# Attention heads of a two-layer trunk: f32 matmuls replaced by three passes on split parts

## The chip, the cores and the metric

The kernel runs on one core of a Trainium2 chip. The metric is the device time of one launch in microseconds. Before the change three runs took 1253.34, 1255.0 and 1253.88 us; the median is 1253.88.

## What is computed

The reference runs two layers over 256 tokens of width 2048. Layer 0 is a Mamba-2 block, layer 1 a sparse attention with a lightning indexer; behind each stands `x = LayerNorm(alpha * x + mixer(x))`. The change touches only the attention of layer 1:

```
q     = (c_q @ w_uq).reshape(b, L, 32, 128)
q_lat = einsum('bthd,hcd->bthc', q, w_uk)
...
logits = einsum('bthc,btkc->bthk', q_lat, kv_sel) * 128 ** -0.5     # selected keys only
pr     = softmax(where(valid, logits, -inf))
o_lat  = einsum('bthk,btkc->bthc', pr, kv_sel)
o      = einsum('bthc,hcv->bthv', o_lat, w_uv).reshape(b, L, 4096)
return (o * silu(gate)) @ w_out
```

There are 32 heads of 128 channels. The kernel computes per head the keys `c_kv @ w_uk` and the values `c_kv @ w_uv`, and a mask stands for the selection.

## The kernel before, in words

The core has a matrix engine (TensorE, PE in the profile; its weight loads are PEld), a vector engine (VectorE, DVE), a scalar engine (ScalarE, ACT), GpSimd (POOL) and a queue of loads (SyncE, SP). Tiles lie in SBUF with 128 partitions. Matmuls write to PSUM, which this kernel divides into eight banks of 512 f32 per partition: three banks tagged `acc`, two `y`, two `m`, one `s`.

All weights pass through one stream of units (class `Stream`, lines 65 to 133). A unit is 128 x 1024 f32 values, loaded by SP into `raw`. ACT copies it to `hi`, rounded to the format fp32r (L98); DVE subtracts, `lo = raw - hi` (L106). Activations are split in the same way. A product is then three single-pass matmuls: hi by hi, hi by lo, lo by hi. `run` (lines 120 to 127) converts up to unit i + 3, issues the matmuls of unit i, and then advances every side generator by one step, older generators first. Each engine executes its instructions in the order in which this loop writes them, so `yield` counts units: a step behind n yields is written n units later. A new tile with the tag of an old one takes the place of one that is no longer used; its writer waits for the last reader of what stood there.

The heads run in 16 pairs. For pair p there are two units and after them units of gates:

- `pair_a` (lines 811 to 831): keys and values of two heads, 12 matmuls each of 256 columns, into two `acc` banks.
- `pair_b` (lines 833 to 844): queries of two heads, 24 matmuls of 256 columns, into a third `acc` bank.
- gates (`add_gate`, line 672, with `stream_w`, line 269): two units per head's gate, 16 matmuls each, into an `acc` bank. `halves` (line 289) takes it out: an ACT copy, and one unit later a DVE addition (L292). The loop at lines 909 to 919 writes one gate after pairs 0, 2, 4, ... and two after pairs 1, 3, 5, ...

So two pairs make ten units. The 32 gates are spread: eight are written before the heads, 24 among them. `gate_steps` (lines 661 to 670) keeps them in a tile with 12 buffers, from the gate's computation to the head that uses it.

`evac_steps` (lines 846 to 851) copies keys, values and queries from PSUM to f32 tiles `hk`, `hv`, `hq` with three buffers each, on ACT, right behind their unit. `head_steps` (lines 853 to 905) is one generator per head. Head 2p starts two units after `pair_b`, head 2p + 1 five units after it:

- its first step: logits in f32, a `y` bank, two matmuls (128 x 128 by L857 and 128 x 256 by L858; the upper right block is masked and left out)
- one unit later: DVE adds the mask and takes the extremum (L866); two: ACT takes the exponential (L871); three: DVE normalises (L874, L876)
- five: TensorE transposes the probabilities to an `m` bank (L882); six: ACT copies them to `prT` (L885)
- eight: outputs in f32, a `y` bank, two matmuls (256 and 128 columns, L889 and L891); nine: DVE multiplies by the gate (L895); then ACT and DVE split the product for the last projection (L902, L904)

Ahead of the heads the indexer's work (lines 748 to 806) lies in an area `sC` of 8192 f32 per partition: latents, indexer queries `qx`, scores `sc` and others, of which lines 1028 to 1039 cut off pieces by `area`. Its last step is the top-k search on DVE (`top_steps`, L793 and L794), which still runs while the first pair of heads is computed. Behind the heads, `x1_steps` (lines 1061 to 1073) loads two rows of gains in pieces into tiles with the tags `hk` and `hq`.

Of the kernel before, what the change touches and what calls it, by code (L numbers as in the profile page):

```python
# [9 lines left out]
F32 = mybir.dt.float32  # L10
F32R = mybir.dt.float32r
I32 = mybir.dt.int32
AF = mybir.ActivationFunctionType
# [3 lines left out]
P = 128  # L17
T = 256
# [29 lines left out]
RAW = 4  # L48
SPLIT = 4
DT_AT = 2  # L50
ON_ACT = 1
EARLY = 8
HELD = 6
# [83 lines left out]
def trunk_kernel(ctx: ExitStack, tc: tile.TileContext, x, xt, w1, wdt, dtp, prm, wo1,  # L137
                 wkv, wcq, wix, wg, wab, wo2, lnr, out):
    nc = tc.nc
# [13 lines left out]
    v = nc.vector  # L153
# [4 lines left out]
    def y_tile(name):  # L158
        return p_y.tile([P, 512], F32, tag="y", name=name)

    def m_tile(name):
        return p_m.tile([P, 512], F32, tag="m", name=name)
# [126 lines left out]
    def halves(dst, ps):  # L289
        nc.scalar.activation(dst, ps[:, T:2 * T], AF.Copy)  # L290
        yield
        v.tensor_add(dst, ps[:, 0:T], dst)  # L292
        yield
# [60 lines left out]
    def m_steps(g, c):  # L354
# [3 lines left out]
        for k in range(2):  # L358
            hh = g * 8 + 2 * c + k
            e = sp3.tile([P, 384], F32, tag="E", name=f"E{hh}")  # L360
            for s, o in ((0, 0), (1, 256)):
                src, dst = a[:, k, s * P:T], e[:, o:o + T - s * P]
                if k < ON_ACT:
                    nc.scalar.activation(dst, src, AF.Relu, scale=-1.0, bias=ask[:, s, hh:hh + 1])  # L364
# [5 lines left out]
        for k, e in enumerate(es):  # L370
            nc.scalar.activation(e, e, AF.Exp, scale=-1.0 if k < ON_ACT else 1.0)
        yield
# [108 lines left out]
    for g in range(NG):  # L481
        for kind, n in (("B", 1), ("C", 1), ("x", 4), ("z", 4)):
            for ci in range(n):
                cell = {"x": xcell}
                for half in range(2):
                    k = len(st.units)
# [71 lines left out]

    st.side(DT_AT, (dt_steps,))
    for g in range(NG):  # L560
# [30 lines left out]
    for kt in range(KT):  # L591
        nc.tensor.matmul(p_dt[0:NH1, 0:T], w_dt[:, kt, :], xr[:, kt, :],
                         start=(kt == 0), stop=(kt == KT - 1))
# [66 lines left out]

    def gate_steps(h, cell):
        ps, d2 = cell["ps"], L["d2"]
        g = d2.tile([P, T], F32, tag="gate", name=f"gate{h}", bufs=12)
        yield from halves(g, ps)
        th = d2.tile([P, T], F32, tag="og", name=f"gth{h}", bufs=3)
        nc.scalar.activation(th, g, AF.Tanh, scale=0.5)
        yield
        v.scalar_tensor_tensor(g, th, 1.0, g, op0=ALU.add, op1=ALU.mult)
        GT[h] = g
        yield  # L670

    def add_gate(h):
        cell = {"x": xcell}
        for half in range(2):
            i = st.add(wg[h * 2 + half], 1024, stream_w(half, cell, f"g{h}"))
        st.side(i, (gate_steps, h, cell))


    A = {}
# [63 lines left out]
    gates = iter(range(NH2))  # L743
# [65 lines left out]
    PR = {}  # L809
# [35 lines left out]

    def evac_steps(p, names):
        for nm in names:
            t = d2.tile([P, 2, T], F32, tag="h" + nm, name=f"h{nm}{p}", bufs=3)
            nc.scalar.activation(t.rearrange("p a b -> p (a b)"), PR[p]["p" + nm], AF.Copy)
            PR[p][nm] = t  # L850
        yield

    def head_steps(h):
        p, k = divmod(h, 2)
        qT, kT, vv = PR[p]["q"][:, k, :], PR[p]["k"][:, k, :], PR[p]["v"]
        pl = y_tile(f"lg{h}")
        nc.tensor.matmul(pl[:, 0:128], qT[:, 0:P], kT[:, 0:P], start=True, stop=True)  # L857
        nc.tensor.matmul(pl[:, 128:384], qT[:, P:T], kT, start=True, stop=True)  # L858
        yield
        lg = d2.tile([P, 384], F32, tag="lg", name=f"lgs{h}")  # L860
        mx = d2.tile([P, 2], F32, tag="mx", name=f"mx{h}")
        sm = d2.tile([P, 2], F32, tag="sm", name=f"sm{h}")
        rn = d2.tile([P, 2], F32, tag="rn", name=f"rn{h}")
        parts = ((0, 0, 128), (1, 128, 384))
        for j, a, b in parts:
            v.tensor_tensor_reduce(out=lg[:, a:b], in0=pl[:, a:b], in1=mb[:, a:b],  # L866
                                   scale=-ATT_SCALE, scalar=3.0e38, op0=ALU.add, op1=ALU.min,
                                   accum_out=mx[:, j:j + 1])
        yield
        for j, a, b in parts:  # L870
            nc.scalar.activation(lg[:, a:b], lg[:, a:b], AF.Exp, scale=-1.0,  # L871
                                 bias=mx[:, j:j + 1], accum_out=sm[:, j:j + 1])
        yield
        v.reciprocal(rn, sm)  # L874
        for j, a, b in parts:
            v.tensor_scalar(lg[:, a:b], lg[:, a:b], rn[:, j:j + 1], 0.5,  # L876
                            op0=ALU.mult, op1=ALU.mult)
        yield
        yield
        pt = m_tile(f"pt{h}")  # L880
        for a in (0, 128, 256):
            nc.tensor.transpose(pt[:, a:a + 128], lg[:, a:a + 128], ident)  # L882
        yield
        prT = d2.tile([P, 384], F32, tag="prT", name=f"prT{h}")
        nc.scalar.activation(prT, pt[:, 0:384], AF.Copy)  # L885
        yield
        yield
        po = y_tile(f"o{h}")
        nc.tensor.matmul(po[:, 0:T], vv[:, 0, k * P:(k + 1) * P], prT[:, 0:256],  # L889
                         start=True, stop=False)  # L890
        nc.tensor.matmul(po[:, P:T], vv[:, 1, k * P:(k + 1) * P], prT[:, 256:384],  # L891
                         start=False, stop=True)
        yield
        og = d2.tile([P, T], F32, tag="og", name=f"og{h}", bufs=3)
        v.tensor_mul(og, po[:, 0:T], GT.pop(h))  # L895
        if h == 0:
            OG.append(big.tile([P, KT, 2 * T], F32R, tag="A", name="og0"))
        if h == 16:
            OG.append(big.tile([P, KT, 2 * T], F32R, tag="C", name="og1"))
        dst = OG[h // 16][:, h % 16, :]  # L900
        yield
        nc.scalar.activation(dst[:, 0:T], og, AF.Copy)  # L902
        yield
        v.tensor_sub(dst[:, T:2 * T], og, dst[:, 0:T].bitcast(F32))  # L904
        yield
# [3 lines left out]
    for p in range(NH2 // 2):  # L909
        src = wab[2 * p]  # L910
        i = st.add(wab[2 * p], 1024, pair_a(p))
        st.side(i, (evac_steps, p, ("k", "v")))
        i = st.add(wab[2 * p + 1], 1024, pair_b(p))
        st.side(i, (evac_steps, p, ("q",)))
        st.side(i + 2, (head_steps, 2 * p))
        st.side(i + 5, (head_steps, 2 * p + 1))
        n = (left * (p + 1)) // 16 - (left * p) // 16
        for _ in range(n):
            add_gate(next(gates))
# [108 lines left out]
    def area(*shape):  # L1028
        n = math.prod(shape)
        t = sC[:, o[0]:o[0] + n]  # L1030
        o[0] += n
        if len(shape) == 2:
            t = t.rearrange("p (a b) -> p a b", a=shape[0])
        elif len(shape) == 3:
            t = t.rearrange("p (a b c) -> p a b c", a=shape[0], b=shape[1])
        return t
    A.update(kv=area(2, 336), q=area(2, 512), wi=area(2, NIX), kd=area(2, P),
             kp=area(T), qx=area(4, 2, T), ra=area(2, 768), sc=area(384),
             cb=area(384))
    nc.gpsimd.memset(A["cb"], 0.0)  # L1040
    for a, w, b in ((0, 128, 0), (128, 256, 128)):
        nc.gpsimd.affine_select(out=A["cb"][:, a:a + w], in_=A["cb"][:, a:a + w],
# [16 lines left out]
    d2 = L["d2"] = heads.enter_context(tc.tile_pool(name="d2", bufs=2))  # L1059

    def x1_steps():

        for n in range(4):
            cs = slice(n * 512, (n + 1) * 512)
            gb = [d2.tile([P, 512], F32, tag=t, name=f"gb{n}_{t}", bufs=3) for t in ("hk", "hq")]
            for k in range(2):
                nc.gpsimd.dma_start(gb[k], lnr[k:k + 1, cs].broadcast_to([P, 512]))
            yield
            for op, w in ((v.tensor_mul, gb[0]), (v.tensor_add, gb[1])):
                for half in range(2):  # L1070
                    r = L["r"][:, half, cs]
                    yield
                    op(r, r, w)
# [58 lines left out]
    L["r"], gbf = fin[:, 0:2, :], fin[:, 2:4, :]  # L1132
    nc.gpsimd.dma_start(fin[:, 0:2, :], x1_d)
    st.side(n_heads + 7, (x1_steps,))
    nc.gpsimd.dma_start(gbf, lnr[2:4, :].rearrange("(o h) t -> o h t", o=1).broadcast_to([P, 2, D]))
    st.run(n_heads + 40)
# [87 lines left out]
```

## Time and profile before

| | |
|---|---|
| median of the runs | 1253.88 us (1253.34 to 1255.0) |
| the profiled execution, device time | 1252.59 us |
| its span, first to last instruction | 1250.8 us |
| mean granted TensorE clock | 0.996 |
| heads among the units, first to last logits | 797.7 to 1063.5 us of the span |

The profile is one execution. A line `L858` is line 858 of the kernel. A row of a group names line, engine, operation, tiles out and in, shape, count, busy time, mean duration of one in ns and the idle time before it. A row of the timeline gives the start, the duration, the engine and the operation. Matmuls are pipelined, so the distance between two starts, not the duration, tells what one costs. An f32 matmul leaves two records, a matmul on fp32r parts one.

### The profile page before, as it was taken

The page shows a single profiled execution, that of the slowest core. Times are in us where ns is not written, and L with a number is a line of the kernel's source. Part 1 is how long each engine was busy: PE and PEld are TensorE (multiplying, and loading weights), DVE is VectorE, ACT ScalarE, POOL GpSimd, SP SyncE. Part 2 cuts the span into 40 slices and gives each one's busy share as a digit, 9 for nine tenths or more (in the row PEclk, how much of TensorE's full clock was granted, in tenths as well). Part 3 has the DMA queues.
Part 4 walks back from the last instruction along what each step waited for, and adds up shares of the span by engine and source line. Part 5 has one row for each costly group of instructions (what it writes and reads, how often), then busy time and mean ns, then how long its engine had stood idle before and what let it go on. Part 6 is the DMA issues. An engine that isn't in the chain of part 4 may idle for free.

```text
span 1250.8 us, 19083 instructions
## 1 busy us (share of the span) xinstructions
PE 1231.4 (98%) x7066; PEld 1069.6 (86%) x7066; DVE 906.9 (72%) x1674; ACT 693.5 (55%) x1188; POOL 67.9 (5%) x104
## 2 busy tenths in 40 slices
PE   8999999999999999999999999999999999999996
PEld 6888888888888888788887898999999999888885
DVE  6978788898898889756457668766666666567457
ACT  5566565666656666544335655566666656443440
POOL 1001001100110011110000000000000000000000
PEclk9999999999999999999999999999999999999998
DMA  7666656575756665676666564544444444965662
GB/s 278 216 182 184 206 179 213 154 221 176 211 169 211 182 212 163 193 237 219 196 193 193 197 205 143 185 155 149 152 152 156 148 152 158 337 214 187 200 199 85
DMA packets 65292, 236.51 MB, mean 189 GB/s; under 512 B 7912, under 2 KB 7920, under 8 KB 64816
## 3 DMA queue, kind: packets, MB, share of 16 engines
q1 hardware_dynamic: 60192, 215.12, 54.0%
q0 software_dynamic: 5008, 20.19, 5.0%
q8 instruction: 55, 0.90, 0.3%
q14 instruction: 37, 0.30, 0.1%
HBM read 231.00 MB, written 4.28 MB: 188 GB/s over the span
## 4 chain that ended last, share of the span: by engine, by line
PE 90%; DVE 6%; ACT 2%; issue 1%; DMA 1%; DVEq 0%; SPq 0%; ACTq 0%
PE acc L285 20%; PE acc L282 10%; PE g L285 9%; PE o L511 9%; PE o L513 9%; PE o L512 9%; PE g L282 5%; DVE lo L106 2%; PE y L409 2%; PE q L840 1%; PE q L842 1%; PE q L841 1%; PE lg L858 1%; PE o L889 1%; PE pt L882 1%
## 5 line engine op out<-in xcount | busy, mean ns | idle before, releaser
L106 DVE TENSOR_TENSOR lo<-raw,hi 128x1024 fp32r<-128x1024 f32 (+1 forms) x404 | 489.6, 1214 | 285.3 <-ACT hi L98 284.8
L98 ACT ACTIVATE hi<-raw 128x1024 fp32r<-128x1024 f32 (+1 forms) x404 | 421.4, 1049 | 220.6 <-PE o L513 158.7
L285 PE MATMUL acc<-xT,hi 128*128 128x512 f32 x1280 | 314.2, 394 | 0.0
L285 PEld LDWEIGHTS acc<-xT,hi 128*128 128x128 f32 x1280 | 233.4, 188 | 45.7 <-ACT E L364 0.9
L282 PEld LDWEIGHTS acc<-xT,lo 128*128 128x128 f32 x1280 | 164.5, 191 | 6.4
L282 PE MATMUL acc<-xT,lo 128*128 128x256 f32 x1280 | 167.9, 283 | 0.0
L285 PE MATMUL g<-x1T,hi 128*128 128x512 f32 x512 | 130.1, 397 | 0.0
L285 PEld LDWEIGHTS g<-x1T,hi 128*128 128x128 f32 x512 | 92.7, 188 | 17.3
L511 PE MATMUL o<-hi,yg 128*128 128x512 f32 x256 | 100.5, 393 | 0.8 <-DVE zs L292 0.8
L513 PE MATMUL o<-hi,yg 128*128 128x512 f32 x256 | 99.7, 389 | 0.0
L512 PE MATMUL o<-lo,yg 128*128 128x512 f32 x256 | 99.6, 389 | 0.0
L511 PE MATMUL o<-hi,og 128*128 128x512 f32 (+1 forms) x256 | 99.4, 388 | 0.0
L513 PE MATMUL o<-hi,og 128*128 128x512 f32 (+1 forms) x256 | 98.8, 386 | 0.0
L512 PE MATMUL o<-lo,og 128*128 128x512 f32 (+1 forms) x256 | 98.8, 386 | 0.0
L282 PE MATMUL g<-x1T,lo 128*128 128x256 f32 x512 | 73.4, 288 | 0.0
L311 DVE SCALAR_TENSOR_TENSOR ca<-cr,convh,ca 128x255 f32<-128x255 f32 x144 | 69.2, 481 | 3.4
L282 PEld LDWEIGHTS g<-x1T,lo 128*128 128x128 f32 x512 | 67.6, 190 | 3.2
L314 ACT ACTIVATE cr<-ca 128x256 f32<-128x256 f32 x48 | 20.1, 418 | 88.4 <-DVE ca L311 88.4
L511 PEld LDWEIGHTS o<-hi,yg 128*128 128x128 f32 x256 | 48.0, 188 | 11.2 <-ACT hi L98 1.3
L513 PEld LDWEIGHTS o<-hi,yg 128*128 128x128 f32 x256 | 48.1, 188 | 10.1
L512 PEld LDWEIGHTS o<-lo,yg 128*128 128x128 f32 x256 | 48.1, 188 | 9.9
L513 PEld LDWEIGHTS o<-hi,og 128*128 128x128 f32 x256 | 48.1, 188 | 9.8
(239 smaller groups left out, 1692.0 us busy)
## 6 DMA issues: line engine op xcount, KB each, us to landing
raw<-in_w_dram SPq DMA_DIRECT2D x160, 512.0 KB, 4.1
raw<-in_wo_dram SPq DMA_DIRECT2D x128, 512.0 KB, 4.1
raw<-in_wg_dram SPq DMA_DIRECT2D x64, 512.0 KB, 3.3
raw<-in_wab_dram SPq DMA_DIRECT2D x32, 512.0 KB, 3.2
abc<-acs_d POOLq DMA_DIRECT2D x32, 256.0 KB, 4.3
raw<-in_wcq_dram SPq DMA_DIRECT2D x8, 512.0 KB, 4.4
raw<-in_wkv_dram SPq DMA_DIRECT2D x8, 336.0 KB, 3.2
rx<-in_x_dram POOLq DMA_DIRECT2D x2, 1024.0 KB, 11.2
```

Source lines behind the costliest of these rows:

```text
L98: self.nc.scalar.activation(h[:, :w], r[:, :w], AF.Copy)
L106: eng.tensor_sub(*self.halfway.pop(i))
L282: nc.tensor.matmul(ps[:, 0:T], l[:, w], xs[:, kt, 0:T], start=False, stop=last, skip_group_check=True)
L285: nc.tensor.matmul(ps, h[:, w], xs[:, kt, :], start=(kt == 0), stop=last, skip_group_check=True)
L311: v.scalar_tensor_tensor(acc[:, d:], rw[:, :T - d], w(k), acc[:, d:], op0=ALU.mult, op1=ALU.add)
L314: nc.scalar.activation(rw, acc, AF.Tanh)
L409: nc.tensor.matmul(py[ks, c * T + s * P:(c + 1) * T], xsT[:, s, c, ks], ms[c][k][:, ws], start=(c == 0 and s == 0), stop=(s == 1), skip_gr ...
L511: nc.tensor.matmul(ps, ah, hs, start=(kk == 2 * first), stop=False)
L512: nc.tensor.matmul(ps, ah, ls, start=False, stop=False)
L513: nc.tensor.matmul(ps, al, hs, start=False, stop=(kk == 31))
L840: nc.tensor.matmul(ps, h[:, o:o + P], cqT[:, kt, 0:T], start=(kt == 0), stop=False)
L841: nc.tensor.matmul(ps, h[:, o:o + P], cqT[:, kt, T:2 * T], start=False, stop=False)
```

## The change

Keys, values, queries and probabilities are taken from PSUM as two fp32r parts: ACT copies the high part, DVE subtracts it from PSUM for the low part. Logits and outputs are then three matmuls on parts in place of each f32 matmul (`mm3`). The part tiles have one buffer (queries), two (keys) and three (values) for each part. To make room, the gates of heads 0 to 15 lie in the indexer's area: six in a piece that was unused, eight over the indexer queries, two over the query latents; the others have seven buffers instead of twelve. The pieces of the gain rows take the tags `hk0` and `hk1` with two buffers.

```diff
+HB = {"q": 1, "k": 2, "v": 3}
...
     def gate_steps(h, cell):
         ps, d2 = cell["ps"], L["d2"]
-        g = d2.tile([P, T], F32, tag="gate", name=f"gate{h}", bufs=12)
+        if h < 16:
+            g = A["gates"][h]
+        else:
+            g = d2.tile([P, T], F32, tag="gate", name=f"gate{h}", bufs=7)
...
         for nm in names:
-            t = d2.tile([P, 2, T], F32, tag="h" + nm, name=f"h{nm}{p}", bufs=3)
-            nc.scalar.activation(t.rearrange("p a b -> p (a b)"), PR[p]["p" + nm], AF.Copy)
+            ps = PR[p]["p" + nm]
+            t = [d2.tile([P, 2, T], F32R, tag=f"h{nm}{k}", name=f"h{nm}{p}_{k}", bufs=HB[nm])
+                 for k in range(2)]
+            hi, lo = (a.rearrange("p a b -> p (a b)") for a in t)
+            nc.scalar.activation(hi, ps, AF.Copy)
+            v.tensor_sub(lo, ps, hi.bitcast(F32))
             PR[p][nm] = t
         yield
+
+    def mm3(ps, a, b, first=True, last=True):
+
+        nc.tensor.matmul(ps, a[0], b[0], start=first, stop=False)
+        nc.tensor.matmul(ps, a[0], b[1], start=False, stop=False)
+        nc.tensor.matmul(ps, a[1], b[0], start=False, stop=last)
...
-        qT, kT, vv = PR[p]["q"][:, k, :], PR[p]["k"][:, k, :], PR[p]["v"]
+        qT, kT = ([a[:, k, :] for a in PR[p][nm]] for nm in "qk")
+        vv = PR[p]["v"]
         pl = y_tile(f"lg{h}")
-        nc.tensor.matmul(pl[:, 0:128], qT[:, 0:P], kT[:, 0:P], start=True, stop=True)
-        nc.tensor.matmul(pl[:, 128:384], qT[:, P:T], kT, start=True, stop=True)
+        mm3(pl[:, 0:128], [a[:, 0:P] for a in qT], [a[:, 0:P] for a in kT])
+        mm3(pl[:, 128:384], [a[:, P:T] for a in qT], kT)
...
-        prT = d2.tile([P, 384], F32, tag="prT", name=f"prT{h}")
-        nc.scalar.activation(prT, pt[:, 0:384], AF.Copy)
+        prT = [d2.tile([P, 384], F32R, tag=f"prT{j}", name=f"prT{h}_{j}") for j in range(2)]
+        nc.scalar.activation(prT[0], pt[:, 0:384], AF.Copy)
+        v.tensor_sub(prT[1], pt[:, 0:384], prT[0].bitcast(F32))
...
-        nc.tensor.matmul(po[:, 0:T], vv[:, 0, k * P:(k + 1) * P], prT[:, 0:256],
-                         start=True, stop=False)
-        nc.tensor.matmul(po[:, P:T], vv[:, 1, k * P:(k + 1) * P], prT[:, 256:384],
-                         start=False, stop=True)
+        mm3(po[:, 0:T], [a[:, 0, k * P:(k + 1) * P] for a in vv], [a[:, 0:256] for a in prT],
+            last=False)
+        mm3(po[:, P:T], [a[:, 1, k * P:(k + 1) * P] for a in vv], [a[:, 256:384] for a in prT],
+            first=False)
...
+    free = area(6, T)
+    A["gates"] = ([free[:, k, :] for k in range(6)] + [A["qx"][:, k // 2, k % 2, :] for k in range(8)]
+                  + [A["q"][:, 0, k * T:(k + 1) * T] for k in range(2)])
...
-            gb = [d2.tile([P, 512], F32, tag=t, name=f"gb{n}_{t}", bufs=3) for t in ("hk", "hq")]
+            gb = [d2.tile([P, 512], F32, tag=t, name=f"gb{n}_{t}") for t in ("hk0", "hk1")]
```

## The prediction

> **What bounds the kernel now.** I read the page first: its busy table and the chain that ended last.
>
> ```profile
> span 1250.8 us, 19083 instructions
> PE 1231.4 (98%) x7066; PEld 1069.6 (86%) x7066; DVE 906.9 (72%) x1674; ACT 693.5 (55%) x1188; POOL 67.9 (5%) x104
> ...
> PE 90%; DVE 6%; ACT 2%; issue 1%; DMA 1%; DVEq 0%; SPq 0%; ACTq 0%
> ```
>
> TensorE is busy for 98% of the span and carries 90% of the chain. The change touches only the stage of the heads, so I asked for that stage by windows: its first pair of heads, the whole stage, and one stretch that repeats (two pairs, four heads).
>
> ```profile
> 786.40:797.70 11.30, 11.30 (x82) 10.62 (x80) 11.06 (x28) 6.54 (x10) 0.00 (x0) 1.00 0.56 177
> 797.70:1060.30 262.60, 262.60 (x1780) 244.06 (x1779) 161.82 (x390) 164.29 (x347) 0.00 (x0) 1.00 0.46 154
> 883.59:918.36 34.77, 34.77 (x239) 32.33 (x238) 21.59 (x52) 21.75 (x46) 0.00 (x0) 1.00 0.47 153
> ```
>
> The columns are the length, then PE, PEld, DVE, ACT, POOL. TensorE has no gap in this stage, its granted clock is 1.00, DVE and ACT are at 62% and 63%. So a microsecond of matmul time that the change adds or removes moves the end by one, and any new wait that reaches TensorE adds to it. In the first window DVE is full (11.06 of 11.30): the top-k search still runs there.
>
> **The matmuls.** The order of time gives the price of each kind by the distance of starts; `x2` means two records for one f32 matmul.
>
> ```profile
> 902.92 0.28 PE L827 MATMUL v<-hi,ckvT 128*128 128x256 f32 x1
> 903.04 0.28 PE L828 MATMUL v<-lo,ckvT 128*128 128x256 f32 x1
> 906.80 0.59 PE L889 MATMUL o<-prT,hv 128*128 128x256 f32 x2
> 907.24 0.38 PE L891 MATMUL o<-prT,hv 128*128 128x128 f32 x2
> 907.46 0.49 PE L882 MATMUL pt<-ident,lgs 128*128 128x128 f32 x3
> ...
> 910.58 0.38 PE L857 MATMUL lg<-hk,hq 128*128 128x128 f32 x2
> 910.80 0.60 PE L858 MATMUL lg<-hk,hq 128*128 128x256 f32 x2
> 911.04 1.30 PE L282 MATMUL g<-x1T,lo 128*128 128x256 f32 x8
> ...
> 914.02 0.39 PE L857 MATMUL lg<-hk,hq 128*128 128x128 f32 x2
> ...
> 917.47 0.59 PE L889 MATMUL o<-prT,hv 128*128 128x256 f32 x2
> ```
>
> A single-pass matmul on split parts, 256 wide, costs 0.12 us (902.92 to 903.04). An f32 matmul costs 0.44 at 256 wide and 0.22 at 128 wide (906.80, 907.24, 907.46). The outputs so cost 0.66. The logits cost 0.64: the next group is recorded 0.46 after them, but 0.18 early, since its eight take 1.30 us where 0.28 and seven steps of 0.12 make 1.12. So a head pays 1.30 us now.
>
> The change puts three single passes for each of these four matmuls: six of 256 wide and six of 128 wide per head. The wide six cost 6 x 0.12 = 0.72. No split-part pass narrower than 256 stands in this trace, so the narrow price is unknown; I bound it with these rows.
>
> ```profile
> 1061.01 0.39 PE L511 MATMUL o<-hi,og 128*128 128x512 f32 x1
> 1061.23 0.39 PE L512 MATMUL o<-lo,og 128*128 128x512 f32 x1
> L409 PEld LDWEIGHTS y<-M,xsT 128*64 128x64 f32 x256 | 15.9, 136 | 10.3 <-issue 5.6
> L840 PEld LDWEIGHTS q<-cqT,hi 128*128 128x128 f32 x128 | 24.4, 191 | 0.2
> ```
>
> Low end: 512 wide costs 0.22 to 0.23 and 256 wide 0.12; halving once more on that line gives 0.066. High end: the f32 price of the same width, 0.22, if narrow passes lose the single-pass rate. Between them: every pass loads its own 128 columns of weights, and a load of 128 columns takes 191 ns where 64 columns take 136, so 64 columns more cost 55 ns and 128 columns hold the loader for 0.11. At 256 wide the load hides behind 0.12 of streaming; at 128 wide it cannot. I take 0.11, because it is read from loads of these very tiles. A head then pays 0.72 + 0.66 = 1.38, 0.08 more than now: 32 x 0.08 = +2.6 us. The ends: 0.066 gives 1.12 a head, -5.8 us; 0.22 gives 2.04, +23.7 us.
>
> The Trainium skill, page "TensorE: Matmul & The Clock Gate", section "Back-to-back issue gap", gives about 81 ns for a sustained 128-wide matmul with its load. By that estimate a head pays 1.21 and the term is -3.0 us instead of +2.6; no run here shows such a pass. The same page's section on LDWEIGHTS, columns divided by 1.2 per ns, speaks against the change: 107 ns for a load of 128 columns, so three narrow passes cost more than the f32 matmul that they replace, as the 55 ns between the two rows above also say.
>
> **The new subtractions** sit on DVE: per pair three of 512 from PSUM, per head one of 384.
>
> ```profile
> L549 DVE SCALAR_TENSOR_TENSOR rx<-rx,o 128x512 f32<-128x512 f32 x8 | 5.4, 676 | 0.0
> L342 DVE TENSOR_TENSOR cbm<-cb,cmask 128x384 f32<-128x384 f32 x8 | 4.4, 546 | 0.0
> L849 ACT ACTIVATE hv<-v 128x512 f32<-128x512 f32 x16 | 9.6, 600 | 17.5 <-PE o L891 10.4 <-PE v L829 7.0
> ```
>
> 6 x 0.68 + 4 x 0.55 = 6.3 us in each stretch of 34.77, so DVE goes from 62% to 80%. As throughput that is hidden. As order it is not, because DVE and ACT run their queues strictly in the order written: each subtraction waits for the ACT copy ahead of it, and a bank or tile of the heads now comes free one DVE step later. ACT's own number of copies is unchanged (L849, L885); only their output type changes. Two places have too little slack.
>
> **Place one:** the query tile has one buffer instead of three. That a copy waits for the last reader of its buffer is seen above: hv, with three buffers, stood 10.4 us for output matmuls L891. With one buffer, the copy of pair p+1's queries waits for the logits of head 2p+1. These are written to start one unit after that copy in every second pair (after a pair followed by one gate).
>
> ```profile
> 906.86 0.42 DVE L895 TENSOR_TENSOR og<-o,gate 128x256 f32<-128x256 f32 x1
> 908.58 1.23 DVE L106 TENSOR_TENSOR lo<-raw,hi 128x1024 fp32r<-128x1024 f32 x1 [1.31 <-ACT hi L98]
> 909.72 0.42 DVE L895 TENSOR_TENSOR og<-o,gate 128x256 f32<-128x256 f32 x1
> ...
> 912.73 0.42 DVE L866 CUSTOM_DVE_ANT_0 lgs<-lg,mb 128x256 f32<-128x256 f32 x1
> ...
> 907.00 0.60 ACT L849 ACTIVATE hq<-q 128x512 f32<-128x512 f32 x1
> 907.50 1.05 ACT L98 ACTIVATE hi<-raw 128x1024 fp32r<-128x1024 f32 x1
> ```
>
> Now the copy starts at 907.00. It will wait until the logits of 910.58 are done (910.80 + 0.60, plus 0.05 for longer passes: 911.45), so it runs 911.5 to 912.1 and its subtraction to 912.7. Behind the copy on ACT is the hi conversion (now 907.50): 912.0 to 913.05. Behind the subtraction on DVE is the lo conversion: 913.1 instead of 908.58, 4.5 late. The multiplication of 909.72 therefore ends at 914.65, and it frees the PSUM tile for the logits at 914.02: two tiles serve logits and outputs in turn. TensorE wants it at 914.1: 0.55 to 0.6 us of stall. The output of 917.47 wants the tile that L866 leaves; that moves from 913.15 to 913.15 + 4.5 + 0.5 (the probabilities' subtraction) = 918.15, and TensorE, itself late, comes at 918.2: nothing. Weights stay ahead: the delayed pair of parts is four units, some 10 us, early. This happens in 8 pairs: 8 x 0.6 = +4.8 us.
>
> **Place two:** the bank that the query projection takes.
>
> ```profile
> 789.22 0.28 PE L840 MATMUL q<-cqT,hi 128*128 128x256 f32 x1
> 791.62 0.42 DVE L292 TENSOR_TENSOR gate<-g,gate 128x256 f32<-128x256 f32 x1
> 889.80 0.47 PE L840 MATMUL q<-cqT,hi 128*128 128x256 f32 x1
> 890.16 0.42 DVE L292 TENSOR_TENSOR gate<-g,gate 128x256 f32<-128x256 f32 x1
> ```
>
> Three banks serve keys, values, queries and gates. In the first pair queries begin at 789.22 although the last gate's addition L292 reads its bank until 792.04: so they stand in the bank that the copy of the keys left. After the change that bank comes free only with the keys' subtraction, which stands behind this L292 on DVE; whichever of the two banks is taken, L292 must be over. In the first pair that costs 792.04 - 789.22 = 2.8 us. In the later even pairs L292 ends at 890.58, TensorE is ready at about 890.04 (889.80, recorded 0.19 early since this one takes 0.47 and not 0.28, and 0.05 for the longer logits before): 0.6 each with the signal, 7 x 0.6 = 4.2. In the odd pairs L292 is over in time. If it is the keys' bank, 0.6 more each, the upper bound (16 x 0.6 = 9.6); if the values' or another bank is free, nothing.
>
> I cost three edits at nothing. Gates 6 to 13 are copied over indexer queries, but the first of them four gate units after the last scores. Seven gate buffers instead of twelve serve the last 16 heads; a gate's copy then waits for a multiplication that is written at least one unit (some 2.9 us) earlier, and without that cover ACT, not TensorE, would wait. The gain rows at the end have two buffers instead of three: a load on GpSimd's queue waits for a multiplication written ten units earlier, and nothing else is queued there.
>
> **Sum.** 2.6 + 4.8 + 2.8 + 4.2 = +14.4 us. The profiled execution took 1252.59 us (span 1250.8 and 1.8 around it) and becomes 1267; the median of the three runs is 1253.88, 1.29 above it, so the forecast is 1268. Bounds of this case: 2.6 to 4.5 for the passes (0.11 to 0.12), 3 (the first pair alone) to 21 (the keys' bank) for the waits: 1259 to 1279.
>
> **Rivals.** (a) Narrow passes fall back to the f32 price, 0.22: +23.7. The longer logits give L292 time (0.25 instead of 0.6), waits 9.4: 1287. For it: nothing below 256 wide is shown; against: from 512 to 256 wide the rate holds. (b) Narrow passes stream at 0.066 and loads don't bind: -5.8, waits 12: 1260. The skill's 81 ns lies between this and mine and gives 1263. Against: the 55 ns. (c) My price for the passes, but the waits find slack (a free bank, a copy that doesn't wait): 1253.88 + 2.6 = 1256.5, a microsecond or two either way. For it: TensorE shows no gap now. (d) Other side: narrow passes at 0.066 and no wait reaches TensorE: 1253.88 - 5.8 = 1248. It decides when a narrow pass is under 0.097 us (0.72 + 6 x 0.097 = 1.30) and the waits stay under the gain.
>
> **Numbers.** Mine 0.55, (a) 0.18, (b) 0.10, (c) 0.12, (d) 0.05. About 0.2% (2.5 us) is what a measurement here can tell from no change. Faster is (d): 0.05. Within 0.2% lies half of (c) and the low edge of (b): 0.09. Slower: 0.86. The range 1256 to 1288 leaves out (d), the lower part of (c) and the upper part of (a), about 0.17.
>
> **What would show it.** The distance of starts of 128-wide passes: 0.11 right; 0.07 or 0.22 the rivals. The odd pairs' query copy should start some 4 us after its matmuls, waiting for logits, with a TensorE gap of about 0.6 us two units later. Queries in the first pair should start near 792. DVE should be near 80% in the repeating stretch. I am wrong if TensorE shows no gaps, or if the extra time lies after the heads.

## The result, and the profile after

The changed kernel takes 1269.45 us (median of 4 runs, 1267.14 to 1270.5); the kernel before takes 1253.61 us beside it (4 runs, 1253.27 to 1255.0). The ratio is 1.0122, with a 95% interval of 1.0104 to 1.0139: slower by 1.2%. The profiled execution took 1269.49 us with a span of 1267.7, which is 16.9 us more span than before. All of it lies in the stage of the heads: from the first matmul of the keys to the first of the last projection 273.98 us became 290.83, and what comes before and after that stage kept its length.

The page of the kernel after, its span, busy table and chain:

```profile
span 1267.7 us, 19451 instructions
...
PE 1237.8 (98%) x7194; PEld 1075.8 (85%) x7194; DVE 949.5 (75%) x1754; ACT 691.5 (55%) x1188; POOL 67.9 (5%) x104
...
PE 84%; DVE 9%; ACT 4%; issue 2%; DMA 1%; SPq 0%; DVEq 0%; ACTq 0%
```

TensorE has 128 matmul records and only 6.4 us of busy time more (an f32 matmul left two records, its three passes leave three). The other ten microseconds are time without a matmul: TensorE's share of the chain fell from 90% to 84%, and DVE's and ACT's rose from 6% and 2% to 9% and 4%. A kernel that was bound by its matmuls now waits in places for the engines that prepare them. The windows of the kernel after say where (length, then busy time of PE, PEld, DVE, ACT, POOL, the granted clock, the DMA share and GB/s):

```profile
788.99:792.09 3.10, 0.28 (x4) 0.11 (x2) 3.03 (x10) 1.66 (x3) 0.00 (x0) 1.00 0.67 235
792.09:797.00 4.91, 4.91 (x27) 4.77 (x27) 3.56 (x9) 0.79 (x2) 0.00 (x0) 0.65 0.40 136
793.42:796.84 3.42, 3.42 (x17) 3.32 (x17) 2.23 (x7) 0.33 (x1) 0.00 (x0) 0.50 0.41 135
802.14:1069.73 267.59, 260.24 (x1851) 241.81 (x1850) 192.96 (x441) 157.35 (x334) 0.00 (x0) 1.00 0.44 144
891.58:928.05 36.47, 35.43 (x255) 32.92 (x254) 26.86 (x63) 21.52 (x47) 0.00 (x0) 1.00 0.43 145
```

The first row is a hole in front of the first pair's queries: 3.10 us with 0.28 of matmul, while DVE is full. The second row was not foreseen: right behind the hole TensorE works without a gap, but at a mean granted clock of 0.65. The third row lies within it and says what that mean is made of: for 3.42 us the clock is 0.50, and before and behind that it is full. The fourth row is nearly all the rest of the stage: 267.59 us long, 260.24 busy, where before had no gap at all. The last row is the repeating stretch of two pairs; it was 34.77 us long, and 1.04 of the 1.70 us that it gained is idle TensorE. DVE is at 26.86 of 36.47, 74%.

The waits of the kernel after in that stage (us in total, times, longest):

```profile
DVE hq L857 <- ACT hq L856: 40.5, 9, 4.9
ACT hq L856 <- PE lg L864: 37.0, 8, 4.7
...
PE q L844 <- DVE sC L293: 3.9, 3, 2.8
PE lg L863 <- ACT hi L99: 3.4, 7, 0.5
PE q L844 <- DVE gate L293: 2.7, 5, 0.5
```

The two large rows cost nothing by themselves: they are ACT and DVE standing idle, 37 us for the one query buffer. What costs is the three small rows, where it is TensorE that waits. The queries L844 wait eight times for the gate's addition L293 (its tile lies in sC for the first 16 heads), once for 2.8 us; the logits L863 wait seven times for 0.5 us.

TensorE's order of time in the kernel after shows the single steps:

```profile
792.09 0.36 PE L844 MATMUL q<-cqT,hi 128*128 128x256 f32 x1 [2.82 <-DVE sC L293]
...
793.11 0.28 PE L846 MATMUL q<-cqT,lo 128*128 128x256 f32 x1
793.23 0.28 PE L844 MATMUL q<-cqT,hi 128*128 128x256 f32 x1
...
793.71 0.41 PE L844 MATMUL q<-cqT,hi 128*128 128x256 f32 x1
793.92 0.41 PE L845 MATMUL q<-cqT,hi 128*128 128x256 f32 x1
...
796.27 2.05 PE L286 MATMUL g<-x1T,hi 128*128 128x512 f32 x7
...
843.01 0.28 PE L863 MATMUL o<-prT,hv 128*128 128x256 f32 x1
843.13 0.28 PE L864 MATMUL o<-prT,hv 128*128 128x256 f32 x1
843.25 0.28 PE L865 MATMUL o<-prT,hv 128*128 128x256 f32 x1
843.37 0.22 PE L863 MATMUL o<-prT,hv 128*128 128x128 f32 x1
843.42 0.28 PE L864 MATMUL o<-prT,hv 128*128 128x128 f32 x1
843.53 0.28 PE L865 MATMUL o<-prT,hv 128*128 128x128 f32 x1
843.65 0.29 PE L897 MATMUL pt<-ident,lgs 128*128 128x128 f32 x1
...
898.99 0.36 PE L844 MATMUL q<-cqT,hi 128*128 128x256 f32 x1 [0.55 <-DVE gate L293]
...
923.85 0.30 PE L863 MATMUL lg<-hk,hq 128*128 128x128 f32 x1 [0.49 <-ACT hi L99]
```

Three things are to be read here. The distance of two 128-wide starts is 0.11 us (843.42 to 843.53). Only the first of the three, right behind a wide pass, takes less, 0.05 (843.37 to 843.42), so the six passes of one output take 0.64 (843.01 to 843.65) and not 0.36 + 0.33 = 0.69. The queries of the first pair step by 0.12 at first and by 0.21 from 793.5 on, so its 24 passes take 4.18 us (792.09 to 796.27) and not 24 x 0.12 = 2.88; the first two steps of the gate behind them are 0.43 and 0.30 instead of 0.23. The low clock thus costs 1.3 + 0.27 = 1.6 us. And in brackets stand the two waits of the repeating stretch, one for the queries, one for the odd pair's logits.

The whole 16.85 us of the stage, by distances of starts in the trace: the odd pairs' logits 7 x 0.65 = 4.5; the even pairs' queries 7 x 0.70 = 4.9; the first pair's hole 2.98 and a small one of 0.27 in the second pair; the low clock 1.6; what is left, 2.6 us or 0.08 a head, is the passes themselves. Part of this too comes with the gaps: the six passes of the logits take 0.77 us behind a gap and 0.69 elsewhere.

### The profile page after: what moved, and what is told of

It reads as the page before. It is cut to its first block, busy times and chain, and to the rows that moved or that the text cites. A ratio compares the mean times of both kernels' runs of the same rounds, so it can differ in the third digit from the quotient of the medians.

```text
span 1267.7 us, 19451 instructions
## 1 busy us (share of the span) xinstructions
PE 1237.8 (98%) x7194; PEld 1075.8 (85%) x7194; DVE 949.5 (75%) x1754; ACT 691.5 (55%) x1188; POOL 67.9 (5%) x104
## 4 chain that ended last, share of the span: by engine, by line
PE 84%; DVE 9%; ACT 4%; issue 2%; DMA 1%; SPq 0%; DVEq 0%; ACTq 0%
PE acc L286 20%; PE acc L283 10%; PE o L512 9%; PE o L513 9%; PE o L514 9%; PE g L286 7%; PE g L283 4%; DVE lo L107 3%; ACT hi L99 2%; PE y L410 2%; PE q L844 1%; PE q L845 1%; PE q L846 1%; PE pt L897 1%; DVE ca L312 1%
```

## The experiments

The theory was that of the prediction: three small causes add up, the passes, the one query buffer (place one), and the query projection's bank (place two). Against it stood three others: DVE at nearly 80% is simply too full, so that gaps move when one is closed; the new places of the gates cost something; the narrow passes are cheaper or dearer than 0.11 and the gaps make up the difference.

**Logits earlier.** In the odd pairs the second head's logits are issued one unit earlier, so that the buffer of the queries comes free before the next copy wants it.

```diff
-        st.side(i + 5, (head_steps, 2 * p + 1))
+        st.side(i + 4, (head_steps, 2 * p + 1))
```

> The changed kernel, with the logits of every odd head written one unit earlier (four units after the queries' unit instead of five), so that they stand ahead of the next pair's query copy and not behind it. My theory: the wait of that copy for the logits (4.7 us each in the changed kernel) goes, and with it the eight gaps of 0.65 us ahead of the second logits: 1269.45 - 5.2 = 1264.3 us. Rival, the gaps come from DVE's load (74% in the repeating stretch) and not from the order: DVE has the same work, so 1268 to 1270.

Measured: 1270.99 us (1269.65 to 1272.08), ratio 1.0144, 1.013 to 1.0158. The number was missed: nothing was gained. TensorE's waits in this kernel, all of the stage's:

```profile
PE q L844 <- DVE gate L293: 5.8, 5, 1.2
PE q L844 <- DVE sC L293: 5.1, 3, 2.8
```

The row of the logits (3.4 us, seven times) is gone as meant, but the queries now wait 10.9 us where they waited 6.6. TensorE's start of the even pairs' queries in this kernel shows it:

```profile
899.58 0.36 PE L844 MATMUL q<-cqT,hi 128*128 128x256 f32 x1 [1.16 <-DVE gate L293]
```

The gap there grew from 0.70 to 1.41 us, by distances of starts. The logits that were moved away, 0.69 us of matmuls, had stood between the values and these queries: they were the cover of place two. One wait was closed and the other was uncovered by as much. This alone can't tell "two causes, one covering the other" from "DVE is too full"; the next two runs do.

**Queries in their own bank.** The queries' projection goes to a pool of one bank that stands unused during the heads, instead of taking turns with keys, values and gates.

```diff
-            pq = acc_tile(f"q{p}")
+            pq = s_tile(f"q{p}")
```

> The changed kernel, with the query projection in the PSUM bank tagged s, which stands unused during the heads, instead of one of the three acc banks. My theory: the queries no longer wait for the gate's addition on DVE, so the first pair's 3.0 us, the slow clock behind it (1.4 us), 0.3 in the second pair and seven gaps of 0.7 us go: 1269.45 - 9.6 = 1259.9 us, with the eight gaps of 0.65 us left. Rival, DVE's load is the cause: 1268 to 1270.

Measured: 1259.07 us (1258.75 to 1259.59), ratio 1.005, 1.0034 to 1.0065, near the 1259.9 expected. Two windows of the first pair in this kernel, the stretch in which the hole stood and the one behind it:

```profile
786.00:792.00 6.00, 6.00 (x50) 5.87 (x49) 5.86 (x17) 3.96 (x7) 0.00 (x0) 1.00 0.58 195
792.00:797.00 5.00, 5.00 (x30) 4.43 (x31) 4.93 (x11) 2.66 (x4) 0.00 (x0) 1.00 0.38 125
```

The hole is gone, with DVE full (5.86 of 6.00), and with the hole the low clock: 1.00 where it was 0.65. TensorE's only wait of this stage is the other one, unchanged:

```profile
PE lg L863 <- ACT hi L99: 3.4, 7, 0.5
```

So the bank is the cause of place two, and the clock's drop came with the hole and not with the new passes.

**Both.** The two edits above together.

> The changed kernel with both edits: odd heads' logits one unit earlier and the queries in the bank of their own. My theory: TensorE has no gap left in the heads, and what remains over the kernel before is the narrow passes' price, about 0.05 us a head or 1.6 us: 1255 us. Rival, DVE's load is the cause: 1268 to 1270. If narrow passes were a gain and only the waits hid it: below 1253.

Measured: 1256.31 us (1255.32 to 1256.98), ratio 1.0027, 1.0016 to 1.0038. The long window of the stage in this kernel:

```profile
802.14:1055.00 252.86, 252.86 (x1815) 238.10 (x1815) 193.69 (x442) 158.61 (x331) 0.00 (x0) 1.00 0.46 152
```

TensorE has no gap, with DVE at 193.69 of 252.86, 77%. The gaps do not need DVE to be less busy in order to go, so "DVE is too full" falls. The earlier logits, worth nothing alone, are worth 2.8 us once the queries have their own bank. What is left, 3.4 us over the kernel before, is the price of the passes. That is 1.3 us more than expected, and TensorE's order of time shows a reason, the logits of two heads:

```profile
846.28 0.27 PE L863 MATMUL lg<-hk,hq 128*128 128x128 f32 x1
...
847.03 2.02 PE L286 MATMUL g<-x1T,hi 128*128 128x512 f32 x8
...
852.96 0.23 PE L863 MATMUL lg<-hk,hq 128*128 128x128 f32 x1
...
853.65 0.28 PE L822 MATMUL k<-ckvT,hi 128*128 128x256 f32 x1
```

With the odd heads one unit earlier, the logits of three heads in four stand right behind the narrow passes of an output and take 0.75 us (846.28 to 847.03); behind wide matmuls they take 0.69 (852.96 to 853.65).

**The narrow third pass twice.** On top of both, the third pass of each 128-wide product is issued twice: 64 passes more.

```diff
         nc.tensor.matmul(ps, a[0], b[1], start=False, stop=False)
+        if b[0].shape[-1] == P:
+            nc.tensor.matmul(ps, a[1], b[0], start=False, stop=False)
         nc.tensor.matmul(ps, a[1], b[0], start=False, stop=last)
```

> As the run with both edits, but each 128-wide product issues its third pass (low part by high part) twice, 64 more narrow passes in all; the low term of those products is counted twice. It prices one narrow pass where nothing else waits: by my 0.11 us each 7.0 us more than the run with both edits, by the streaming rate of 0.066 us 4.2 more, by the f32 rate of 0.22 us 14 more.

Measured: 1263.05 us (1262.66 to 1263.38), ratio 1.0081, 1.0067 to 1.0094. That is 6.74 us over the kernel with both edits, 0.105 us for each of 64 passes: what a load of 128 columns takes by the two rows of loads in the prediction (55 ns for 64 columns), and neither 0.066 nor 0.22. That it is the load that sets this price is argued from this match and from the single step of 0.05 shown above, right behind a wide pass; no run varies the load alone.

**Narrow products in f32.** If a narrow pass is bound by its load, three of them (0.33) lose to the two records of one f32 matmul (0.22), and three wide ones (0.36) beat theirs (0.44). So the wide products keep the three passes, and the narrow ones go back to f32, with an f32 copy of the columns they need. The parts shrink by that, which makes room for two query buffers; the queries have their own bank, and the logits stay where the changed kernel has them.

```diff
-HB = {"q": 1, "k": 2, "v": 3}
+HB = {"q": 2, "k": 2, "v": 3}
...
-            pq = acc_tile(f"q{p}")
+            pq = s_tile(f"q{p}")
...
+            nc.scalar.activation(t[0], cut, AF.Copy)
+            nc.scalar.activation(f, full, AF.Copy)
+            v.tensor_sub(t[1], cut, t[0].bitcast(F32))
...
-        mm3(pl[:, 0:128], [a[:, 0:P] for a in qT], [a[:, 0:P] for a in kT])
-        mm3(pl[:, 128:384], [a[:, P:T] for a in qT], kT)
+        nc.tensor.matmul(pl[:, 0:128], PR[p]["qf"][:, k, :], PR[p]["kf"][:, k, :], start=True,
+                         stop=True)
+        mm3(pl[:, 128:384], qT, kT)
...
-        mm3(po[:, P:T], [a[:, 1, k * P:(k + 1) * P] for a in vv], [a[:, 256:384] for a in prT],
-            first=False)
+        nc.tensor.matmul(po[:, P:T], PR[p]["vf"][:, 0, k * P:(k + 1) * P], prf, start=False,
+                         stop=True)
```

> The changed kernel with the queries in a bank of their own, two buffers for the query tiles and the order of logits as it was, and with the 128-wide products in f32 again: f32 copies of the columns that they need are taken from PSUM by ACT beside the parts, which shrink accordingly. A head then pays 2 x (3 x 0.12 + 0.22) = 1.16 us where the kernel before pays 1.30, and no wait should reach TensorE: by my prices 32 x 0.14 = 4.5 us less than the kernel before, 1248 to 1249 us. If the two buffers don't take the place of the earlier logits, eight gaps of 0.65 us come back: 1253 to 1254. If the narrow products were not what cost time: as the run with both edits, 1256.

Measured: 1248.51 us (1248.27 to 1249.07) beside 1253.08 for the kernel before, ratio 0.9963, 0.995 to 0.9977. It beats both kernels. Its long window, and one output of a head in TensorE's order of time:

```profile
802.00:1050.00 248.00, 248.00 (x1766) 233.16 (x1766) 183.72 (x446) 164.28 (x403) 0.00 (x0) 1.00 0.45 157
```

```profile
906.09 0.28 PE L870 MATMUL o<-prT,hv 128*128 128x256 f32 x1
906.21 0.28 PE L871 MATMUL o<-prT,hv 128*128 128x256 f32 x1
906.33 0.28 PE L872 MATMUL o<-prT,hv 128*128 128x256 f32 x1
906.45 0.38 PE L916 MATMUL o<-prf,hv_f 128*128 128x128 f32 x2
906.67 0.49 PE L905 MATMUL pt<-ident,lgs 128*128 128x128 f32 x3
```

The output takes 0.36 + 0.22 = 0.58 us (906.09 to 906.67), 0.66 before the change. A head pays 1.16 instead of 1.30, and 32 x 0.14 = 4.5 us is what the run gained: 4.6.

**Before, with the gates' new places.** The kernel before with only that edit: the first 16 gates copied over the indexer's area, seven buffers for the rest.

```diff
-        g = d2.tile([P, T], F32, tag="gate", name=f"gate{h}", bufs=12)
+        if h < 16:
+            g = A["gates"][h]
+        else:
+            g = d2.tile([P, T], F32, tag="gate", name=f"gate{h}", bufs=7)
...
```

> The kernel before, with nothing but the places of the gates changed: heads 0 to 15 in the indexer's area, seven buffers for the others. My theory: no cost, 1252 to 1254 us. Rival, the area or the fewer buffers make copies wait: more than 1 us slower.

Measured: 1253.47 us (1252.31 to 1254.6) beside 1253.08, ratio 1.0002, 0.9993 to 1.001. The places cost nothing that can be measured.

**Before, with one query buffer.** The kernel before, in f32 and without any subtraction, but with one buffer for the queries. The second gain row at the end takes the values' tag in place of the queries'.

```diff
-            t = d2.tile([P, 2, T], F32, tag="h" + nm, name=f"h{nm}{p}", bufs=3)
+            t = d2.tile([P, 2, T], F32, tag="h" + nm, name=f"h{nm}{p}", bufs=1 if nm == "q" else 3)
...
```

> The kernel before, with one buffer for the f32 query tiles instead of three and nothing else that matters (the second gain row takes the values' tag). There are no subtractions and DVE stays at 62%. My theory: ACT's copy waits some 4 us for the odd head's logits in eight pairs, the weight conversion behind it and DVE's multiplication behind that come 4.4 us late, and the second logits stall 0.5 to 0.6 us: 4 to 5 us slower, 1257 to 1258. Rival, it takes the subtractions as well: 1253.

Measured: 1258.79 us (1258.5 to 1259.42) beside 1253.08, ratio 1.0046, 1.0034 to 1.0059: 5.7 us, a little over the expected 4 to 5. Seven gaps stand in its trace, each 0.76 us by starts. One odd pair of this kernel in the order of time, first ACT, then DVE, then TensorE:

```profile
913.37 0.60 ACT L849 ACTIVATE hq<-q 128x512 f32<-128x512 f32 x1 [4.63 <-PE lg L858]
```

```profile
914.95 1.23 DVE L106 TENSOR_TENSOR lo<-raw,hi 128x1024 fp32r<-128x1024 f32 x1 [5.80 <-ACT hi L98]
916.10 0.42 DVE L895 TENSOR_TENSOR og<-o,gate 128x256 f32<-128x256 f32 x1
```

```profile
916.66 0.46 PE L857 MATMUL lg<-hk,hq 128*128 128x128 f32 x2 [0.60 <-DVE rn L874]
```

The query copy waits for the odd head's logits, the hi conversion stands behind it on ACT, the lo conversion waits for that on DVE, the multiplication L895 stands behind lo and ends at 916.52, and the logits come right behind it. (The profile names L874 as the releaser, the next instruction on DVE, which ended last; the logits read nothing of it.) So place one needs neither the subtractions nor the three passes: the single query buffer is enough. Two query buffers at full size in the changed kernel were not tried: they ask for more of a partition's memory than it has left.

## Where the prediction was right and where not

**The sign, the size and the three causes.** 1268 was said and 1269.45 measured; all three causes were there, in the places named, and nothing lies outside the heads. By what the edits take back (differences of ratios, times 1253): place two with the low clock 0.0122 - 0.0050, 9.0 us; place one 0.0050 - 0.0027, 2.9; passes 0.0027, 3.4. Predicted were 7.0, 4.8 and 2.6. By the length of the stage in the traces (290.83, 280.59, 277.48 and 273.98 us) the three are 10.2, 3.8 and 2.8; there the 0.69 us is counted off by which the run with both edits has the last head's logits ahead of the stage's end and not behind it. Either way place two was sized too low and place one too high. The total was closer than its terms, and that closeness is luck.

**The passes.** The 0.11 read from the loads was right: 0.105 by the doubled pass, 0.11 by starts. The choice of the loads' row over the halved streaming time decided the sign of this term, and the measured price rules out rivals (a), (b) and (d). The Trainium skill, page "TensorE: Matmul & The Clock Gate", gives columns divided by 1.2 per ns for LDWEIGHTS, by estimate 107 ns for 128; the 0.105 and 0.11 us here agree. The 81 ns of its section "Back-to-back issue gap" is not what these 128-wide passes reach. What the term left out is that a price depends on the neighbours: a head pays 0.64 for the outputs and 0.69 for the logits, or 0.75 where the logits stand right behind narrow passes, so 1.33 to 1.39 where 1.38 was said. In the repeating stretch of the run with both edits that makes 35.15 us (902.12 to 937.27, from logits to logits) where 34.77 were: 0.38 in four heads, 3.0 us in all. Its median is 3.4 over the kernel before; in the two traces the rest lies ahead of the heads, which begin at 787.01 us there and at 786.35 before.

**Place one.** The chain was as worked out. In the changed kernel, ACT's order of time and DVE's in an odd pair:

```profile
920.57 0.60 ACT L856 ACTIVATE hq<-q 128x512 fp32r<-128x512 f32 x1 [4.72 <-PE lg L864]
921.06 1.05 ACT L99 ACTIVATE hi<-raw 128x1024 fp32r<-128x1024 f32 x1
```

```profile
921.20 0.69 DVE L857 TENSOR_TENSOR hq<-q,hq 128x512 fp32r<-128x512 f32 x1 [4.94 <-ACT hq L856]
922.15 1.23 DVE L107 TENSOR_TENSOR lo<-raw,hi 128x1024 fp32r<-128x1024 f32 x1 [0.26 <-ACT hi L99]
923.29 0.42 DVE L911 TENSOR_TENSOR og<-o,sC 128x256 f32<-128x256 f32 x1
```

The copy waits 4.72 us, the subtraction and lo follow it, the multiplication ends at 923.71 and the logits start at 923.85. The profile names ACT's hi as their releaser, because another hi ended last, at 923.74; the logits read nothing of it, and the multiplication 0.03 earlier is the one in the chain. That is argued from the code; shown is that the gaps go with the copy's wait. A gap costs 0.65 by starts, a little over the 0.6 that was said, but there are seven: the first odd pair has none. Taken back they bring 2.9 us, not 4.5. The traces give two reasons. The edit that closes a gap also moves logits behind narrow passes, where they cost more, so the repeating stretch falls from 35.68 us (own bank alone, 901.53 to 937.21) to 35.15 (both edits): 0.53 a gap, 3.7 in all. And the heads begin 1.0 us later in the trace of the run with both edits (787.01 against 786.02), ahead of anything that the edit touches.

**Place two.** The first pair's queries started at 792.09, as the prediction had it ("near 792"). DVE's order of time in the changed kernel tells which bank it was, in the first pair and in an even one:

```profile
791.53 0.42 DVE L293 TENSOR_TENSOR sC<-g,sC 128x256 f32<-128x256 f32 x1
791.86 0.68 DVE L857 TENSOR_TENSOR hk<-k,hk 128x512 fp32r<-128x512 f32 x1
...
898.42 0.42 DVE L293 TENSOR_TENSOR gate<-g,gate 128x256 f32<-128x256 f32 x1
898.76 0.68 DVE L857 TENSOR_TENSOR hk<-k,hk 128x512 fp32r<-128x512 f32 x1
```

The queries start 0.14 and 0.15 us after L293 ends (791.95, 898.84), while the keys' subtraction is still running (to 792.54 and 899.44). So it is the gate's bank, the one taken for the forecast, and not the keys', the upper bound. The even pairs' gaps are 0.70, not 0.60.

**What failed in the sum** is the first pair's term: 2.8 was right for the hole (2.98), but a hole of that length had a price of its own, the lower clock behind it, 1.6 us. No row of the kernel before showed TensorE idle for that long in this stage, and the prediction priced only the wait. With 0.18 more for the hole, 0.27 in the second pair and 0.1 more in each even one, that makes place two 2.7 us dearer by starts than forecast (2.0 by what the edit takes back). One odd pair fewer, and gaps worth 0.53 rather than 0.6, hid part of it in the total.

**DVE's share** was said to become 80% of the stretch and is 74%. The stretch has 11 instructions more (63 against 52; ten are the subtractions), but they add 5.27 us and not 6.3, since neighbouring records overlap (the gate's addition above ends at 791.95, the subtraction behind it begins at 791.86); and the stretch itself is longer. The conclusion, that DVE's throughput isn't the limit, held, and the run with both edits shows it at 77%.

**Costed at nothing.** The gates' places were right at nothing (ratio 1.0002). The gain rows' buffers at the end were not tried alone; the tail's length did not change.

Rival (c), no wait reaching TensorE, gave 1256.5 for the kernel with the prices of the forecast and no gaps. The run with both edits is that kernel: 1256.31, or 1.0027 of its kernel before where (c) makes 1.0021.

## What to carry to other kernels

Price a matmul that is split into passes at each of its widths: here three passes win at 256 wide (0.36 against 0.44) and lose at 128 wide (0.28 to 0.33 against 0.22), since a narrow pass costs what the load of its weights does, and the better kernel splits only the wide products. Where an operand gains a second part, ask of every buffer and bank that it touches which instruction now frees it, and what stands ahead of that instruction in its engine's queue. A wait that is closed by moving work may have been the cover of the next one, so close both before judging either.

## What the runs showed of the hardware that was not expected

A hole of 2.98 us in TensorE's work was followed by 3.42 us at a granted clock of 0.50 (793.42 to 796.84; steps of 0.12 until 793.2, 0.21 from 793.5). The drop began 1.3 us after the work had begun again. In the run with the earlier logits the queries of the first pair start at 791.77 behind a hole of the same size, and there it began 0.4 us before them:

```profile
791.39:794.80 3.41, 3.02 (x14) 3.06 (x15) 3.38 (x8) 0.42 (x1) 0.00 (x0) 0.50 0.23 89
```

So the length of the drop was the same in both, and its start was not tied to the work's. With the hole closed the clock stays at 1.00. The gaps of 0.5 to 1.4 us elsewhere, up to fourteen in a run, left it at 1.00. The Trainium skill, page "TensorE: Matmul & The Clock Gate", Part 1, tells of a free-running window of about 3.4 us whose idleness lowers the clock; the drop agrees, but it came with a hole somewhat shorter than that.
